# Mixer of a decoder trunk: the loads that bring queries and keys back are issued by SP instead of GpSimd

## The chip, the cores and the metric

The kernel runs on one core of one Trainium2 chip. The metric is the device time of one execution in microseconds (us). The core has a matrix engine (PE; its weight loads are listed apart as PEld), a vector engine (DVE), a scalar engine (ACT), a general engine (GpSimd, listed as POOL) and SP, which computes nothing and issues transfers. Each engine works through its own list of instructions in order, and an instruction that waits holds up everything behind it on that engine. A transfer is issued by SP, ACT or POOL and then carried out by the core's 16 DMA engines; the issuer goes on at once, and a semaphore tells when the data has landed. What SP issues stands in the profile as queue q1 (hardware descriptors), what POOL issues as queue q0 (software descriptors).

## The reference

Two layers (DEPTH = 2) over x of 512 tokens by 1024 channels. Each layer is a half-step SwiGLU, a token mixer, and a second half-step SwiGLU, each followed by a layer norm. The mixer projects x by w_in and has three head groups, all causal:

```
aq, ak, av, bq, bk, bv, cc = split(x @ w_in[l])
o_a = rms_norm(diff_attention(rope(aq), rope(ak), av, lam))      # 6 heads, two maps of 32 channels each
o_b = rms_norm(dilated_attention(rope(bq), rope(bk), bv))        # 6 heads of 64 channels
o_c, v_first = rwkv7_mixer(cc, ...)                              # 4 heads, a recurrence over the tokens
x = layer_norm(ALPHA * x + concat(o_a, o_b, o_c) @ w_out[l])
```

diff_attention takes the softmax of two score maps per head and subtracts lam times the second from the first. All is float32.

## The kernel before, in words

Products are kept near float32 precision by splitting every operand into a rounded part (hi) and a remainder (lo) and adding three matmuls (`mm3`). Weights are loaded by SP (tiles `wr`, two buffers, in the mixer), split by ACT (`wh`) and POOL (`wl`), eight buffers each.

The mixer is written as streams (`RANK` lists them), Python generators that emit instructions piece by piece. A planner, `Board.merge`, keeps an estimated clock for each engine and always continues the stream that can run first by that estimate; so the order on every engine is fixed when the program is built, and the estimated cost of a transfer's issue (1.04 us on POOL, 0.47 us on SP) shifts it. The streams near the change are these.

`columns` projects x. For queries and keys it goes by pairs of heads: three pairs of group A, three of group B. A pair is projected for four tiles of 128 tokens and rotated.

`turner` transposes each such tile on PE, splits it into hi and lo in a tile `z` (ACT writes one part, DVE the other; `z` has two buffers), and SP stores it to DRAM (`qkA` or `qkB`, one tensor per pair). Four stores make a pair complete.

`fetch` (lines 769 to 798) loads a pair back, head by head (e = 0, 1), rearranged so that one matmul reaches hi and lo products together. A head of group A takes four loads: 64 partitions of `q` and 64 of `k` (256 KB each), whose source is two blocks of 32 rows, hi and lo or one of them twice; and 32 partitions of `q` and of `k` (128 KB each) from one block. A head of group B takes two loads into the two halves of `q` (256 KB each, 128 partitions, source two blocks of 64 rows) and one of 64 partitions into `k` (128 KB). The tiles `q` and `k` share four buffers (tag `x`), so two heads can be held at a time. The first head of a group also loads the mask (`bias`).

`attend` computes the scores of 24 units per group (three pairs, two heads, four query tiles): PE makes `p<-k,q`, DVE adds the mask and takes the maximum, ACT the exponential, PE transposes and multiplies with the values. It frees a head's `q` and `k` after the head's fourth unit.

`inside`, `invert`, `scan` and `rwkv_out` do the recurrence. `inside` sends its small blocks through DRAM on SP's queue (`ub`, then `tt` to `td` and back); `scan` loads `kr` on SP.

Of the kernel before, what the change touches and what calls it, by code (L numbers as in the profile page):

```python
# [520 lines left out]
class Mix:  # L521
# [246 lines left out]

    def fetch(self):

        dma = self.gps.dma_start
        ap = lambda t, off, dims: bass.AP(tensor=t.tensor, offset=t.offset + off, ap=dims)
        for grp in "AB":
            for hp in range(3):
                for e in range(2):
                    yield f"qk{grp}{hp}", "x", "x"
                    if (hp, e) == (0, 0):
                        yield f"qk{grp}{hp}", "x", "x", "bias"
                        self.bias = self.get("bias", "bias")
                        dma(self.bias, self.tr.consts[:, 130:642] if grp == "A" else self.tr.consts[:, 642:1154])  # L780
                    a = self.get("x", "q", (128, 2, S))
                    d = self.qk[grp, hp]
                    hi, lo, k = e * 64 * S, (256 + e * 64) * S, 128 * S
                    if grp == "A":
                        b = self.get("x", "k", (128, 2, S))
                        dma(a[0:64], ap(d, hi, [[256 * S, 2], [2 * S, 32], [1, 2 * S]]))
                        dma(b[0:64], ap(d, hi + k, [[0, 2], [2 * S, 32], [1, 2 * S]]))
                        dma(a[64:96], ap(d, hi, [[2 * S, 32], [1, 2 * S]]))
                        dma(b[64:96], ap(d, lo + k, [[2 * S, 32], [1, 2 * S]]))
                    else:  # L790
                        b = self.get("x", "k2", (64, S))
                        dma(a[:, 0, :], ap(d, hi, [[256 * S, 2], [S, 64], [1, S]]))
                        dma(a[:, 1, :], ap(d, hi + k, [[0, 2], [S, 64], [1, S]]))
                        dma(b, ap(d, lo + k, [[S, 64], [1, S]]))
                    self.qkt[grp, hp, e] = a.bitcast(FR), b.bitcast(FR)
                    self.mark(f"q{grp}{hp}{e}")
# [753 lines left out]
```

## Time and profile before

| what | value |
|---|---|
| runs | 2336.46, 2327.51, 2321.31 us; median 2327.51 us |
| the profiled execution's own time | 2319.83 us |
| its span, first to last instruction | 2318.0 us |
| PE / DVE / ACT / POOL busy | 96% / 49% / 35% / 14% |
| mean granted TensorE clock | 0.975 |
| mixer of layer 0, attention in it | about 385 to 815 us, 490 to 720 us |
| mixer of layer 1, attention in it | about 1532 to 1970 us, 1642 to 1875 us |

Times in the trace count from the span's start. A wait of an engine costs time only where nothing else was ready behind it in that engine's order, and on PE nearly every wait does. The profile lists for each transfer when it was issued and when it landed.

### The profile page before, as it was taken

What the parts mean: (1) busy time and instruction counts of PE and PEld (TensorE: products, weight loads), DVE (VectorE), ACT (ScalarE), POOL (GpSimd) and SP (SyncE); (2) the same over time, 40 slices, a digit from 0 to 9 for tenths busy, and PEclk for the clock granted to TensorE, in tenths of its full rate; (3) what the DMA queues carried; (4) which work ended last, traced back from release to release, by engine and by line L of the source; (5) the groups of instructions that cost most, each with busy time, mean ns of one, the idle gap of its engine ahead of it and who ended that gap; (6) DMA issues with size and microseconds to landing.
All of it is one profiled execution on the core that took longest, in us unless ns stands there. A gap on an engine that the chain in (4) does not pass through costs nothing.

```text
span 2318.0 us, 31736 instructions
## 1 busy us (share of the span) xinstructions
PE 2215.6 (96%) x12384; PEld 1863.6 (80%) x12384; DVE 1146.8 (49%) x2483; ACT 803.4 (35%) x1559; POOL 317.5 (14%) x344
## 2 busy tenths in 40 slices
PE   9999999988899999999999999999878999999998
PEld 8888888787776788888888888887877867888886
DVE  3333346766566633333653332656765666333336
ACT  4322223435444323222433222343444443222222
POOL 1000002343232200000010000033432322000000
PEclk9999999999899999999999999999987999999999
DMA  5333344354433323332543333432553323233334
GB/s 171 101 102 98 113 137 146 102 136 98 104 106 101 118 74 94 98 99 91 173 120 108 101 96 109 155 128 85 136 108 94 107 95 119 84 98 91 100 109 154
DMA packets 253030, 258.34 MB, mean 111 GB/s; under 512 B 45562, under 2 KB 202304, under 8 KB 252880
## 3 DMA queue, kind: packets, MB, share of 16 engines
q1 hardware_dynamic: 221488, 228.20, 32.4%
q0 software_dynamic: 30816, 27.06, 4.8%
q8 instruction: 97, 1.59, 0.3%
q10 hardware_dynamic: 576, 1.05, 0.1%
q14 instruction: 53, 0.43, 0.1%
HBM read 233.85 MB, written 22.28 MB: 110 GB/s over the span
## 4 chain that ended last, share of the span: by engine, by line
PE 80%; DVE 8%; DMA 5%; issue 4%; POOL 1%; ACT 1%; SPq 0%; POOLq 0%; DVEq 0%; ACTq 0%
PE p L87 18%; PE p L86 18%; PE p L85 18%; PE p L511 13%; PE m L511 4%; PE r L511 3%; DMA k<-qkA 3%; PE r L86 2%; PE r L85 2%; PE r L87 2%; DMA k<-qkB 1%; DVE x L511 1%; POOL wl L511 1%; DMA q<-qkB 0%; DVE x L146 0%
## 5 line engine op out<-in xcount | busy, mean ns | idle before, releaser
L80 DVE TENSOR_TENSOR lo<-raw,hi 128x1024 fp32r<-128x1024 f32 x300 | 366.2, 1223 | 627.8 <-ACT hi L79 627.5
L87 PE MATMUL p<-xhi,lo 128*128 128x512 f32 (+1 forms) x1392 | 535.7, 385 | 0.0
L86 PE MATMUL p<-xlo,hi 128*128 128x512 f32 (+1 forms) x1392 | 533.7, 383 | 0.7 <-DVE xlo L126 0.7
L85 PE MATMUL p<-xhi,hi 128*128 128x512 f32 (+1 forms) x1392 | 533.6, 383 | 0.5 <-ACT xhi L125 0.5
L79 ACT CAST hi<-raw 128x1024 fp32r<-128x1024 f32 x300 | 315.6, 1053 | 583.5 <-PE p L86 258.1
L86 PEld LDWEIGHTS p<-xlo,hi 128*128 128x128 f32 x1392 | 261.7, 188 | 56.3 <-DVE xlo L126 1.1
L85 PEld LDWEIGHTS p<-xhi,hi 128*128 128x128 f32 x1392 | 261.8, 188 | 53.8 <-ACT xhi L125 1.0
L87 PEld LDWEIGHTS p<-xhi,lo 128*128 128x128 f32 x1392 | 261.9, 188 | 52.6
L511 POOL TENSOR_TENSOR wl<-wr,wh 128x512 fp32r<-128x512 f32 x152 | 203.8, 1360 | 670.1 <-ACT wh L511 629.3
L511 PE MATMUL p<-wh,xhi 128*128 128x256 f32 (+1 forms) x704 | 233.7, 332 | 1.4 <-DVE rb L511 1.1
L511 PE MATMUL p<-wh,xlo 128*128 128x256 f32 (+1 forms) x704 | 218.9, 311 | 0.5 <-DVE xlo L511 0.4
L511 PE MATMUL p<-wl,xhi 128*128 128x256 f32 (+1 forms) x704 | 218.5, 310 | 0.0
L87 PE MATMUL p<-hi,hl 128*128 128x512 f32 x528 | 205.8, 390 | 0.0
L86 PE MATMUL p<-lo,hh 128*128 128x512 f32 x528 | 205.8, 390 | 0.0
L85 PE MATMUL p<-hi,hh 128*128 128x512 f32 x528 | 205.7, 390 | 0.0
L511 PEld LDWEIGHTS p<-wh,xhi 128*128 128x128 f32 x704 | 138.9, 197 | 12.7 <-PE p L511 1.5
L511 PEld LDWEIGHTS p<-wh,xlo 128*128 128x128 f32 x704 | 138.7, 197 | 7.6 <-DVE xlo L511 2.2
L246 DVE TENSOR_TENSOR hr<-p,hr 128x512 f32<-128x512 f32 x88 | 60.8, 691 | 167.3 <-PE p L87 156.9
L511 PEld LDWEIGHTS p<-wl,xhi 128*128 128x128 f32 x704 | 139.2, 198 | 4.3
L247 ACT CAST hh<-hr 128x512 fp32r<-128x512 f32 x88 | 54.3, 617 | 205.9 <-DVE hr L246 195.8
L511 ACT ACTIVATE t<-t,nm 128x128 f32<-128x128 f32 (+3 forms) x144 | 80.2, 557 | 125.0 <-DVE nm L511 124.0
L85 PEld LDWEIGHTS p<-hi,hh 128*128 128x128 f32 x528 | 99.1, 188 | 20.6
(253 smaller groups left out, 3061.0 us busy)
## 6 DMA issues: line engine op xcount, KB each, us to landing
raw<-in_ffn_a_down SPq DMA_DIRECT2D x66, 512.0 KB, 3.3
raw<-in_ffn_b_down SPq DMA_DIRECT2D x66, 512.0 KB, 3.3
raw<-in_ffn_a_gate SPq DMA_DIRECT2D x44, 512.0 KB, 3.8
raw<-in_ffn_a_up SPq DMA_DIRECT2D x44, 512.0 KB, 3.9
raw<-in_ffn_b_gate SPq DMA_DIRECT2D x40, 512.0 KB, 3.9
raw<-in_ffn_b_up SPq DMA_DIRECT2D x40, 512.0 KB, 3.8
wr<-in_w_in SPq DMA_DIRECT2D x56, 256.0 KB, 3.1
wr<-in_w_in SPq DMA_DIRECT2D x24, 512.0 KB, 3.8
```

What stands on the lines that cost most here:

```text
L79: nc.scalar.copy(hi, raw)
L80: (vec or nc.vector).tensor_tensor(lo, raw, hi.bitcast(FT), op=OP.subtract)
L85: mm(out, lh, rh, start=first, stop=False)
L86: mm(out, lh, rl, start=False, stop=False)
L87: mm(out, ll, rh, start=False, stop=last)
L246: nc.vector.tensor_tensor(hr, acc[1, f], hr, op=OP.mult)
L247: nc.scalar.copy(hi, hr)
L511: return call(*args, **kw)
```

## The change

The loads of `fetch` are issued by SP on its hardware queue. The mask load stays on GpSimd. All addresses, sizes and buffers are the same.

```diff
     def fetch(self):
 
-        dma = self.gps.dma_start
+        dma = self.sp.dma_start
...
                         self.bias = self.get("bias", "bias")
-                        dma(self.bias, self.tr.consts[:, 130:642] if grp == "A" else self.tr.consts[:, 642:1154])
+                        self.gps.dma_start(self.bias, self.tr.consts[:, 130:642] if grp == "A" else self.tr.consts[:, 642:1154])
```

The 42 loads of a layer move from POOL's list to SP's, and since the planner counts less for them, the order of the other streams shifts around them. Three places follow; the number behind a name tells one use of a buffer from the next.

SP in layer 0, around the first pair of group A, before: stores of the second pair (`qkA0_1`), then the recurrence's trip through DRAM (`td0`, `td`).

```order
L511 DMA qkA0_1_2685<-z_3877 128x4x128
L511 DMA qkA0_1_2685<-z_3951 128x4x128
L511 DMA qkA0_1_2685<-z_4003 128x4x128
L511 DMA td0_4051<-tt_3586 128x16x16 x2
L511 DMA td_4050<-td0_4051 128x1x256 x2
```

The same place now:

```order
L511 DMA q_3939<-qkA0_0_2684 64x1x1024
L511 DMA k_3940<-qkA0_0_2684 64x1x1024
L511 DMA q_3939<-qkA0_0_2684 32x1024
L511 DMA k_3940<-qkA0_0_2684 32x1024
L511 DMA q_3945<-qkA0_0_2684 64x1x1024
L511 DMA k_3946<-qkA0_0_2684 64x1x1024
L511 DMA q_3945<-qkA0_0_2684 32x1024
L511 DMA k_3946<-qkA0_0_2684 32x1024
L511 DMA qkA0_1_2685<-z_3951 128x4x128
L511 DMA wr_4021<-in_w_in 128x4x128 x2
L511 DMA qkA0_1_2685<-z_4003 128x4x128
L511 DMA td0_4069<-tt_3586 128x16x16 x2
```

Both heads of the pair are issued in one go, ahead of the second and third store of the next pair, a weight load and the recurrence's trip.

ACT in layer 0, between the third and the fourth unit of that pair's first head (`t` are the units' exponentials, `aT` a transposed unit, `wh` weights), before:

```order
L511 COPY aT_4125<-m_4123 128x128
L511 CAST wh_4142<-wr_3904 128x512
L511 CAST wh_4146<-wr_3904 128x512
L511 ACTIVATE t_4159,l_4156<-t_4159,nm_4160 128x512
L511 ACTIVATE t_4165,l_4156<-t_4165,nm_4166 128x512
```

and now:

```order
L511 COPY aT_4131<-m_4129 128x128
L511 CAST z_4133<-m_4134 128x256
L511 COPY v_4044<-p0_4046 128x2x128
L511 ACTIVATE t_4162,l_4159<-t_4162,nm_4163 128x512
L511 ACTIVATE t_4168,l_4159<-t_4168,nm_4169 128x512
```

The fourth tile of the second pair, `z_4133`, is now written ahead of the fourth unit's exponentials; before it (as `z_4183`) came behind them. It takes the buffer of `z_3951`, whose store stands right behind the eight loads on SP.

SP in layer 0, from the second to the third pair of group B, now (before, SP had the stores and the weights alone, and POOL the loads):

```order
L511 DMA qkB0_2_2689<-z_6344 128x4x128
L511 DMA q_6382<-qkB0_1_2688 128x1x512 x2
L511 DMA k2_6383<-qkB0_1_2688 64x512
L511 DMA q_6387<-qkB0_1_2688 128x1x512 x2
L511 DMA k2_6388<-qkB0_1_2688 64x512
L511 DMA qkB0_2_2689<-z_6415 128x4x128
L511 DMA qkB0_2_2689<-z_6469 128x4x128
L511 DMA wr_6531<-in_w_out 128x2x512
L511 DMA qkB0_2_2689<-z_6541 128x4x128
L511 DMA wr_6607<-in_w_out 128x2x512
L511 DMA q_6633<-qkB0_2_2689 128x1x512 x2
L511 DMA k2_6634<-qkB0_2_2689 64x512
```

Here the second store of the third pair, `z_6415`, stands right behind two heads' loads; the fourth, `z_6541`, takes its buffer.

## Rows read from the trace of the kernel before

**Rows 1.** Page, section 1, PE: busy us (share of span), instructions.

```profile
PE 2215.6 (96%) x12384; PEld 1863.6 (80%) x12384; DVE 1146.8 (49%) x2483; ACT 803.4 (35%) x1559; POOL 317.5 (14%) x344
```

**Rows 2.** Waits of PE, 385 to 815 us: us in total, times, longest.

```profile
PE p L511 <- DMA k<-qkA: 18.1, 3, 8.6
PE p L511 <- DMA q<-qkB: 1.7, 2, 1.2
```

**Rows 3.** Waits of PE, 1532 to 1970 us.

```profile
PE p L511 <- DMA k<-qkA: 20.6, 3, 11.5
```

**Rows 4.** Windows: stretch, length, engines' busy us, granted clock, DMA share, GB/s.

```profile
490.00:720.00 230.00, 199.93 (x1761) 177.56 (x1761) 149.77 (x561) 111.89 (x378) 73.67 (x85) 0.91 0.43 112
506.00:509.00 3.00, 2.98 (x14) 3.00 (x15) 1.20 (x7) 1.10 (x5) 0.00 (x0) 0.50 0.45 92
```

**Rows 5.** Timeline of PE: start, duration, instruction, count [idle before <- releaser].

```profile
506.02 0.76 PE L511 MATMUL p<-k,q 96*128 96x256 f32 x2 [3.50 <-DMA k<-qkA]
...
515.90 0.40 PE L511 MATMUL p<-k,q 96*128 96x256 f32 x2
...
545.05 0.77 PE L511 MATMUL p<-k,q 96*128 96x256 f32 x2 [8.60 <-DMA k<-qkA]
...
703.25 0.35 PE L511 MATMUL p<-q 128*128 128x256 f32 x1
```

**Rows 6.** Chain that ended last: start, us, what (a transfer runs from issue to landing).

```profile
494.42 11.35 DMA k<-qkA
...
528.26 16.54 DMA k<-qkA
...
576.00 12.29 DMA k<-qkA
...
704.07 8.25 DMA k<-qkB
```

**Rows 7.** Timeline of POOL: its issues of the loads (start, us, count).

```profile
492.56 0.69 POOL L511 DMA_DIRECT2D q<-qkA  x1 [1.57 <-issue]
...
526.40 0.72 POOL L511 DMA_DIRECT2D q<-qkA  x1
...
670.64 1.62 POOL L511 DMA_DIRECT2D q<-qkB  x2 [3.70 <-DMA qkB<-z]
...
694.13 1.62 POOL L511 DMA_DIRECT2D q<-qkB  x2 [1.53 <-PE m L511]
...
702.47 1.62 POOL L511 DMA_DIRECT2D q<-qkB  x2 [6.16 <-PE m L511]
```

**Rows 8.** DMA issues, whole program: issuer, count, KB each, median us to landing.

```profile
q<-qkB POOLq DMA_DIRECT2D x24, 256.0 KB, 9.3
...
ub<-am SPq DMA_DIRECT2D x64, 4.0 KB, 1.5
```

**Rows 9.** Windows while a head of group B is loaded; columns as in rows 4.

```profile
700.00:701.00 1.00, 1.00 (x10) 0.90 (x8) 0.34 (x5) 0.98 (x5) 0.00 (x0) 1.00 0.26 102
701.00:702.00 1.00, 1.00 (x7) 0.61 (x5) 0.28 (x1) 0.59 (x2) 0.00 (x0) 1.00 0.26 102
```

**Rows 10.** DMA issues, 492 to 497 us; columns as in rows 8.

```profile
qkA<-z SPq DMA_DIRECT2D x2, 256.0 KB, 12.3
q<-qkA POOLq DMA_DIRECT2D x2, 256.0 KB, 11.1
```

**Rows 11.** Timeline of SP: start, us from the first issue to the last.

```profile
511.06 1.77 SPq L511 DMA_DIRECT2D td<-td  x2
...
518.16 0.37 SPq L511 DMA_DIRECT2D qkA<-z  x1
...
689.98 0.36 SPq L511 DMA_DIRECT2D qkB<-z  x1
```

**Rows 12.** Timeline of ACT around the first pair's units.

```profile
500.18 0.37 ACT L511 CAST z<-m 128x256 fp32r<-128x256 f32 x1 [3.64 <-DMA qkA<-z]
...
512.28 0.24 ACT L511 COPY aT<-m 128x128 f32<-128x128 f32 x1
```

## The prediction, made before the result was known

> **What bounds the kernel now.** I read the busy table first [rows 1]: PE is busy 96% of the span, so time can only come from, or go into, stretches where PE stands still or runs at half clock. Then PE's waits inside the two mixers [rows 2, 3]: of all that PE waits for there, the loads this change moves are the largest item, 18.1 + 1.7 us in layer 0 and 20.6 us in layer 1. The attention stretch [rows 4] shows the frame, in its first row: PE busy 199.93 of 230 us at a mean clock of 0.91. The timeline of PE [rows 5] shows where the waits stand: 3.50 us before the first head of group A, 8.60 us before the third; in layer 1 the longest is 11.5 us [rows 3]. After such a wait the granted clock stays at 0.50, the lower of its two levels (1.2 of 2.4 GHz), for about 3 us [rows 4], the second row, which costs some 1.5 us more. Last the chain of waits [rows 6]: every link that is a load of this kind runs 8 to 17 us from issue to landing. So the loads' latency matters, and whatever makes the first head of a pair land earlier or later moves the kernel almost one for one.
>
> **Price of one load.** While one head of group B is being loaded, two big pieces of 256 KB move, and the DMA share stands at 0.26 with 102 GB/s [rows 9]. 0.26 of 16 engines is 4.2 engines: two per big piece, each at 102/4.2 = 24.5 GB/s. So the pieces whose source is two blocks go through two engines only, and one takes 262 KB / (2 x 24.5 GB/s) = 5.35 us. On POOL's queue the two pieces use different engines and run side by side. A 128 KB piece, spread over 16 engines, takes 131 KB / (16 x 24.5) = 0.33 us. What remains of the 9.3 us landing [rows 8] is 3.95 us of start and landing on POOL's queue; SP's smallest transfers land in 1.5 us [rows 8], which I take as start and landing there.
>
> No row shows which engines SP's queue gives to a two-engine piece. The bounds: always the same pair, so that pieces run one after another, or a different pair each, as on POOL's queue. I take the same pair, since every other SP transfer of this kernel starts from a fixed split and nothing in the trace shows SP's queue rotating. The Trainium skill, DMA: Bandwidth & Descriptors, section Why a DMA increments its semaphore by 16 and not by 1, says that a hardware-queue transfer uses as many engines as divide the slowest dimension on both sides, and always the lowest-numbered ones, while the software queue moves a cursor on. By that rule two-block pieces all meet on two engines; no run here shows it yet.
>
> Head of group B on SP: 2 x 5.35 + 0.33 + 1.5 = **12.5 us**, against 702.47 to 712.32 = 9.85 us now [rows 6, 7]; spread it would be 7.2 us. Head of group A: one big piece takes between 5.35 us and 11.1 - 3.95 = 7.15 us [rows 8, 10], two small ones 0.66: 12.9 to 16.5 us, and I take **14 us**, nearer the lower end, since the upper was measured with eight pieces in flight. Now: 492.56 to 505.77 = 13.2 us for the first head and 526.40 to 544.80 = 18.4 us for the third [rows 6, 7]. A second head issued at once lands 11 (B) to 12.5 us (A) after the first. So the first head of a pair comes about as late as today; what changes is how long the two engines stay taken: 26 us for a pair. Every other SP transfer is spread over all the engines, those two included, and lands only when they are free. Today such a store already takes 12.3 us behind a pair [rows 10].
>
> **The sum, layer 0.**
> 1. First pair (A). First head +0.8 us. Second head lands at 492.6 + 26.5 = 519, needed at 515.90 [rows 5]: up to +3. The store of `z_3951` stands behind the pair and lands near 520; ACT's `z_4133` needs that buffer, and in the new order it comes right behind the copy that ends at 512.5 [rows 12]. ACT stands there until 520, where it now waits at most 3.64 us, with the fourth unit's exponentials behind it: **+6.6 us**, which covers the other two.
> 2. Second pair, first head. The recurrence's loads, now issued at 511.06, follow a store that lands near 520, so go out near 521; the fourth store, now at 518.16 [rows 11], at about 524, landed at 526. So the load is issued when it is today, 526, but lands at 540 instead of 544.80. PE, 6.6 us late, would arrive there at 543 and finds it: the 8.60 us wait goes. Shift so far 6.6 - 8.6 = -2; some wait is likely left, so **-1 us**. In layer 1, with 11.5 us to absorb, -4.
> 3. Third pair: 12.29 us plus 1.86 for the three issues ahead of it [rows 6, 7] is 14.1 now, 14 then: 0. A held store there: +1.
> 4. First pair of B: its first head comes up to 12.5 - 9.85 = 2.7 us later; today's PE waits for such loads are 1.7 us in all [rows 2], so most of it lies beside other work: +0.5.
> 5. Second and third pair of B. The third pair's fourth tile uses the buffer of a store that stands behind two B heads issued at 670.64; these hold the engines until 670.64 + 1 + 22 = 694, landing near 696 instead of today's store time of 689.98 [rows 7, 11]. The third pair is then complete near 699.5 rather than 694: its first head lands at 712 against 703.66, its second, behind it on the same two engines, at 722 against 712.3. PE needs the first at 703.25 [rows 5]: **+10 us**.
>
> Layer 0: -1 + 1 + 0.5 + 10 = +10.5; layer 1: +7.5. The profiled execution took 2319.83 us and would take 2338; it lies 7.7 us under the median of the runs, so the forecast is 2327.5 + 18 = **2346 us**. POOL's part: it loses 42 issues of 0.5 to 0.8 us a layer, beside idle time (14% busy), so 0. SP gains them at about 0.4 us; what stands behind is told above. The mask load stays on POOL and costs nothing new.
>
> **Rivals.**
> A, faster: SP's queue gives each piece its own engines. A head of A then lands in 5.35 to 7.15 + 0.66 + 1.5 = 7.5 to 9.3 us, of B in 7.2. That is 4 to 9 us under today, which takes nearly all of the 18.1 + 1.7 and 20.6 us and about 9 us of half-clock time: up to -49. With a third lost to the next wait (PE idles for a dozen other releasers too), -33: 2294 us. For it: those waits end last on PE. Against: nothing in the trace shows a rotation on SP's queue. Chance 0.17. The Trainium skill, same page, section Issuing engine by pattern, recommends SP for simple loads; by that advice this case would be the likely one, and nothing measured here supports it for two-block pieces.
>
> B, clearly slower: stores and weights held behind the pairs decide. A pair of A at the upper price takes 2 x (14.3 + 0.66) + 1.5 = 31 us, and four pairs a layer each hold the third or fourth next `z` (two buffers), `td`, `kr` and `wr` by 10 to 19 us more than the 12.3 of today. If one such hold of 8 us is waited for at each of the four pairs, it is 4 x 8 x 2 = +64: 2392 us. It decides when the tile two stores on is due within some 25 us of a pair's issue; today's stores come 5 to 20 us apart. Chance 0.33.
>
> C, nothing: the lost latency and the absorbed waits cancel: 2327. Chance 0.15. My forecast, mild loss: 0.35, own range 2330 to 2362.
>
> **Numbers.** About 1% (23 us) is what a measurement of this kernel tells from no change. Faster by more: nearly all of A, 0.15. Slower by more (over 2351): B and 0.4 of the forecast, 0.47. The same: 0.38. The range leaves out the better half of A and the upper end of B: 2298 to 2396.
>
> **What would show it.** After the change, in the windows while a head is loaded and nothing else moves, a DMA share near 0.13 (two engines) for twice as long proves the shared pair; 0.26 proves rival A. Landing times of q and k: 6 to 12 us staggered within a head (shared), or all near 8 (spread). The `z`, `wr` and `td` transfers behind a pair landing after 20 us or more. PE's wait before the third head of A gone or small, ACT's wait for `z` near 515 us, a later fetch and a PE wait in the third pair of B. If ACT and PE never wait for these stores, steps 1 and 5 are wrong and C or A remains; if PE's waits for `k<-qkA` grow, my 14 us is too low.

## The result, and the profile after

The changed kernel takes 2403.64 us (median; 2400.95 to 2408.03) beside 2326.45 us for the kernel before on the same chip: a ratio of 1.033, 95% interval [1.029, 1.037]. It is slower by 77 us where 18 were forecast, and lies above the range. The profiled execution took 2405.72 us, its span is 2403.9 us against 2318.0, and the mean granted clock 0.945 against 0.975. The busy row of the page, beside [rows 1]:

```profile
PE 2266.4 (94%) x12384; PEld 1905.5 (79%) x12384; DVE 1138.5 (47%) x2483; ACT 806.8 (34%) x1559; POOL 261.2 (11%) x260
```

The same 12384 multiplications keep PE busy 50.8 us longer, and the rest of the span, in which PE stands idle, grew from 102.4 to 137.5 us. So of the 85.9 us between the two spans (the medians differ by 77), **35 are waiting and 51 are slower work**. Added up over the clock's records, PE's clock was at the lower level for 109 us in 16 stretches before and for 259 us in 26 after. PE was busy in 88 us of the former and in 202 us of the latter; at 1.00 in place of 0.50 half of that time would do, so the difference is worth 57 us by this estimate, and the clock accounts for all of the slower work.

The waits of all engines in the mixer of layer 0 (385 to 860 us of the changed kernel), those that a DMA ends, beside [rows 2]; then PE's longest in layer 1 (1582 to 2056 us), beside [rows 3]:

```profile
PE p L511 <- DMA k<-qkA: 19.6, 3, 6.9
PE p L511 <- DMA q<-qkB: 15.7, 4, 5.6
ACT z L511 <- DMA qkB<-z: 7.4, 1, 7.4
...
ACT z L511 <- DMA qkA<-z: 4.7, 1, 4.7
```

```profile
PE p L511 <- DMA k<-qkA: 23.0, 3, 8.1
```

Group A's waits are about what they were; group B's went from 1.7 to 15.7 us in layer 0 and are 1.5 us in layer 1. The waits of ACT for a store (`qkA<-z`, `qkB<-z`) go on to PE, since the copy that PE needs stands behind `z` in ACT's list. Two waits of PE in layer 0 and one in layer 1 come from this; in the kernel before they are 0.7 us or nothing:

```profile
PE m L511 <- ACT aT L511: 5.7, 1, 5.7
PE p L511 <- ACT v L511: 3.1, 1, 3.1
...
PE m L511 <- DVE z L511: 6.8, 1, 6.8
```

So of the 35 us of waiting about 19 are loads (40.4 us for q and k in both mixers before, 59.8 after) and about 16 are held stores. The attention stretch of layer 0 in the windows, beside [rows 4], and the one of layer 1:

```profile
495.00:762.00 267.00, 218.78 (x1757) 195.08 (x1758) 144.54 (x560) 113.87 (x378) 44.95 (x43) 0.81 0.31 96
```

```profile
1692.00:1956.00 264.00, 220.22 (x1760) 194.15 (x1760) 148.94 (x565) 114.64 (x380) 47.84 (x44) 0.82 0.32 98
```

They take 267 us where it took 230 and 264 where it took 233, and PE's clock stands at 0.81 on average in layer 0 where it stood at 0.91. Two windows of 1 us in which nothing but heads moves (last two columns: DMA share, GB/s), beside the 0.26 and 102 GB/s of [rows 9]:

```profile
514.00:515.00 1.00, 1.00 (x7) 1.00 (x6) 0.04 (x1) 0.46 (x3) 0.00 (x0) 0.50 0.13 53
...
703.00:704.00 1.00, 0.00 (x0) 0.00 (x0) 0.98 (x2) 0.00 (x0) 0.13 (x1) 0.50 0.13 51
```

A share of 0.13 is two of 16 engines, at 53 and 51 GB/s: one piece at a time, 262 KB / 51 GB/s = 5.1 us each. The forecast of the shared pair holds, and so does its price. SP's own timeline (start, duration, instruction), first pair of group A from its fifth load on:

```profile
499.79 0.51 SPq L511 DMA_DIRECT2D q<-qkA  x1
500.40 3.06 SPq L511 DMA_DIRECT2D k<-qkA  x1
503.50 4.95 SPq L511 DMA_DIRECT2D q<-qkA  x1
508.50 0.88 SPq L511 DMA_DIRECT2D k<-qkA  x1
509.48 0.38 SPq L511 DMA_DIRECT2D qkA<-z  x1
512.03 7.83 SPq L511 DMA_DIRECT2D wr<-in_w_in  x2
519.95 0.46 SPq L511 DMA_DIRECT2D qkA<-z  x1
520.50 6.25 SPq L511 DMA_DIRECT2D td<-tt  x2
```

Here is something that the forecast did not have, and an issuer does not always go on at once: the sixth and the seventh load's issue take 3 and 5 us instead of 0.4 to 0.6. SP stands in its own issues while the two engines work off what is queued, and so does everything behind it in SP's list. By the semaphore events the pair issued from 497.57 us on landed at 512.59 (first head) and 523.98 (second), 15.0 and 26.4 us after its issue began, and the store of `z_3951`, issued at 509.48, at 524.69.

PE's timeline where it waits for a head in layer 0, beside [rows 5] (start, duration, instruction, idle time before it and what ended it):

```profile
512.63 0.80 PE L511 MATMUL p<-k,q 96*128 96x256 f32 x2 [6.74 <-DMA k<-qkA]
...
550.53 0.77 PE L511 MATMUL p<-k,q 96*128 96x256 f32 x2 [5.91 <-DMA k<-qkA]
...
608.36 0.55 PE L511 MATMUL p<-k,q 96*128 96x256 f32 x1 [6.94 <-DMA k<-qkA]
...
660.63 0.55 PE L511 MATMUL p<-q 128*128 128x256 f32 x1 [4.58 <-DMA q<-qkB]
...
706.79 0.55 PE L511 MATMUL p<-q 128*128 128x256 f32 x1 [4.97 <-DMA q<-qkB]
...
750.29 0.55 PE L511 MATMUL p<-q 128*128 128x256 f32 x1 [5.56 <-DMA q<-qkB]
```

Cut at the first scores of the same heads, and taken from the windows view of both kernels, layer 0 reads:

| stretch of layer 0 (us in it, PE busy) | before | after | more idle | more busy |
|---|---|---|---|---|
| mixer's start to first head of A | 121.0, 110.3 | 125.6, 112.2 | 2.7 | 1.9 |
| first to third head of A | 39.0, 28.8 | 37.9, 28.9 | -1.3 | 0.1 |
| third to fifth head of A | 43.5, 37.5 | 57.8, 50.2 | 1.6 | 12.7 |
| fifth of A to first of B | 42.2, 38.6 | 40.5, 39.5 | -2.5 | 0.8 |
| first to third head of B | 53.6, 50.9 | 57.9, 46.7 | 8.6 | -4.2 |
| third to sixth head of B | 27.5, 25.9 | 43.5, 32.3 | 9.6 | 6.4 |
| sixth head of B to the end | 103.2, 94.5 | 111.7, 102.3 | 0.7 | 7.8 |

The planner moved work between neighbouring stretches, so single rows mix both effects; the sums, 19.3 us more idle and 25.7 us more busy, don't. The last two stretches of the kernel before and then of the changed one (length; busy time of PE, PEld, DVE, ACT, POOL; granted clock):

```profile
684.34:711.81 27.47, 25.85 (x180) 19.75 (x178) 18.28 (x83) 20.48 (x70) 10.68 (x12) 1.00 0.37 109
711.81:815.00 103.19, 94.49 (x559) 77.31 (x560) 70.46 (x194) 35.02 (x81) 24.91 (x23) 0.98 0.34 110
```

```profile
706.79:750.29 43.50, 32.29 (x142) 24.91 (x143) 12.82 (x56) 19.14 (x65) 3.57 (x4) 0.70 0.34 110
750.29:862.00 111.71, 102.33 (x558) 84.34 (x559) 70.74 (x189) 35.22 (x79) 25.04 (x23) 0.88 0.29 93
```

In the first of them PE does fewer multiplications (142 against 180) in more busy time, at a clock of 0.70 instead of 1.00. In the last it does the same work, 558 against 559, and takes 7.8 us longer for it at 0.88 instead of 0.98.

### The profile page after: what moved, and what is told of

Read it like the earlier page. It is cut to its first block, busy times and chain, and to the rows that moved or that the text cites. A ratio compares the mean times of both kernels' runs of the same rounds, so it can differ in the third digit from the quotient of the medians.

```text
span 2403.9 us, 31738 instructions
## 1 busy us (share of the span) xinstructions
PE 2266.4 (94%) x12384; PEld 1905.5 (79%) x12384; DVE 1138.5 (47%) x2483; ACT 806.8 (34%) x1559; POOL 261.2 (11%) x260
## 4 chain that ended last, share of the span: by engine, by line
PE 80%; DVE 9%; DMA 6%; issue 2%; SPq 2%; ACT 1%; POOL 0%; DVEq 0%; ACTq 0%; POOLq 0%
PE p L87 17%; PE p L86 17%; PE p L85 17%; PE p L511 14%; PE r L511 5%; PE m L511 4%; DMA q<-qkB 2%; SPq L511 2%; PE r L86 2%; PE r L87 2%; PE r L85 2%; DMA qkA<-z 1%; DMA qkB<-z 1%; DVE x L511 1%; DMA k<-qkA 1%
## 5 line engine op out<-in xcount | busy, mean ns | idle before, releaser
L511 PE MATMUL p<-wh,xhi 128*128 128x256 f32 (+1 forms) x704 | 240.1, 341 | 6.6 <-ACT v L511 3.1
L511 PEld LDWEIGHTS p<-wh,xlo 128*128 128x128 f32 x704 | 142.7, 203 | 8.5 <-DVE xlo L511 2.9
L86 PEld LDWEIGHTS p<-lo,hh 128*128 128x128 f32 x528 | 99.1, 188 | 20.5
```

Of the source, the lines that this page charges most:

```text
L86: mm(out, lh, rl, start=False, stop=False)
L511: return call(*args, **kw)
```

## The experiments

The theories: **T1**, a piece whose source is two blocks moves through two engines, on SP's queue always the same two, and that makes the heads of a pair late and holds what is queued behind. **R1**, the loss is the planner's other order (it counts 0.47 us for an issue on SP, 1.04 on GpSimd). **R2**, SP's queue is slower for such loads whatever their source. **R3**, the number of loads or the order made of it decides. **T2**, the granted clock carries the larger part of the loss.

**The split on SP.** Each two-block load becomes two loads of one block, for group A (`b` and group B likewise):

```diff
-dma(a[0:64], ap(d, hi, [[256 * S, 2], [2 * S, 32], [1, 2 * S]]))
+dma(a[0:32], ap(d, hi, [[2 * S, 32], [1, 2 * S]]))
+dma(a[32:64], ap(d, lo, [[2 * S, 32], [1, 2 * S]]))
```

> The changed kernel, but each piece whose source is two blocks is written as two loads of one block each (six loads per head of group A, five per head of B, all on SP's queue). T1 (each two-block piece goes through two engines, all pieces through the same two, so that a pair of heads takes 26 us there, holds SP's other transfers and stops SP's issues): a head lands in 3 to 5 us, SP's stores are held no longer, PE's waits for q and k in layer 0 (35.3 us in the changed kernel) fall under 8, and the time falls below the kernel before: 2270 to 2310 us. R1 (the other order that the planner makes of it costs the time): the order is nearly as in the changed kernel, so it stays near 2400. R2 (SP's queue or its in-order waits are what is slow, whatever the source): near 2400, or more by the added issues.

Measured: 2271.81 us, ratio to before 0.976 [0.972, 0.979]: 5.5% under the changed kernel and faster than both. The transfers of 495 to 760 us (KB each, median us to landing):

```profile
q<-qkB SPq DMA_DIRECT2D x24, 128.0 KB, 2.7
qkA<-z SPq DMA_DIRECT2D x9, 256.0 KB, 3.7
q<-qkA SPq DMA_DIRECT2D x18, 128.0 KB, 4.9
k<-qkA SPq DMA_DIRECT2D x18, 128.0 KB, 4.8
```

PE waits for no load of q or k in either mixer. R2 is out, for more loads go through the same queue. R1 and R3 are not, as the order differs.

**One block, the same loads, on SP.** In the changed kernel only the source patterns are altered; the rows behind the first block are read in place of the second block:

```diff
-dma(a[0:64], ap(d, hi, [[256 * S, 2], [2 * S, 32], [1, 2 * S]]))
+dma(a[0:64], ap(d, hi, [[2 * S, 64], [1, 2 * S]]))
```

> The changed kernel with the same number, size and order of loads on SP, but the source of each two-block piece is one block of as many rows (it reads the rows behind the block in place of the second block, so what is computed of the scores is other data). T1 (two engines for a two-block source, all pieces on the same two): the pieces go to all the engines, a head lands in 3 to 5 us, the time is that of the split, 2265 to 2290. R3 (the split gained by its finer loads or by the order that the planner makes of more loads, not by the engines): above 2330.

Measured: 2266.98 us, ratio 0.973 [0.968, 0.978]. The lists of PE, DVE, ACT and POOL are the changed kernel's word for word; only the pattern of the source differs, and it is worth 137 us. R3 is out. Busy row and transfers, 495 to 760 us:

```profile
PE 2206.7 (97%) x12384; PEld 1856.2 (82%) x12384; DVE 1137.8 (50%) x2483; ACT 802.6 (35%) x1559; POOL 262.2 (12%) x260
```

```profile
q<-qkB SPq DMA_DIRECT2D x12, 256.0 KB, 3.3
...
q<-qkA SPq DMA_DIRECT2D x6, 256.0 KB, 5.0
k<-qkA SPq DMA_DIRECT2D x6, 256.0 KB, 5.5
```

Of the 132.6 us between the spans (2403.9 and 2271.3), 59.7 are busy time and 72.9 idle time.

**One block on GpSimd.** The same edit in the kernel before.

> The kernel before, loads on GpSimd's queue as they are in number, size and order, but the source of each two-block piece is one block of as many rows (other rows are read, so what is computed of the scores is other data). PE's waits for q and k should vanish as they did in the split on GpSimd's queue. T1 with idle time alone: the 29 us of PE's idle time that the split on that queue took away come off, without its added issues: 2285 to 2305. T2 (the granted clock takes back what the waits give, as in that split, where PE's busy time rose by 39 us): 2320 to 2350, with 170 us or more at the lower clock.

Measured: 2273.59 us, ratio 0.976 [0.971, 0.981], better than T1's own figure; T2's warning was wrong here, the time at the lower clock fell to 68 us. With sources of one block the two queues cannot be told apart (2267 and 2274). The orders differ between these two runs; in one and the same order, split loads take 2347 us on GpSimd's queue and 2348 on SP's (the split in the other orders, below). The two-block source costs 55 us on GpSimd's queue and 137 on SP's: **the change made an old flaw dearer**, it did not bring a new one.

**Order and queue apart.** The first keeps the changed order with GpSimd as issuer, the second the order of before with SP:

```diff
-dma = self.sp.dma_start
+dma = Watched(self.board, "sp", self.nc.gpsimd).dma_start
```

```diff
-dma = self.gps.dma_start
+dma = Watched(self.board, "pool", self.nc.sync).dma_start
```

> The changed kernel's order of the work (the planner counts the loads as SP's), but the loads are issued by GpSimd on its own queue, as before. T1: within 12 us of the kernel before, 2315 to 2340. R1 (the order costs it): most of the 77 us is here, 2380 to 2405. R2: as T1.

> The order of the kernel before (the planner counts the loads as GpSimd's), but SP issues them on its hardware queue. T1: the pair of engines decides, so most of the loss is here: 2380 to 2420. R1: near 2327. R2: 2380 to 2420 as T1; what tells R2 from T1 is the split of the sources, not this run.

Measured: 2345.27 us, ratio 1.007 [1.004, 1.011], for the order alone, and 2370.68 us, 1.016 [1.011, 1.020], for the queue alone, both just outside T1's figures. So the order costs 18 us with the loads on GpSimd and 33 with them on SP; the queue 43 in the old order and 58 in the new one. R1 holds some of the loss, though not as R1 has it: with one-block sources the new order is not slower (2267 against 2274). There is no one price for an order: below, split loads on SP take 2272 us in one order and 2348 in another, with no head late in either.

**Group A or group B alone split**, on SP (edits as in the split, in one branch):

> The changed kernel with the split (one block to a load) in group A alone; the heads of group B still go through two engines. By the split of both groups (2272) and none (2404) there are 132 us to share. T1, by where the shifts stand in the profile of the changed kernel (about half in group A's heads, half in group B's): 2325 to 2350. By the prediction's steps (group B's second and third pair carry the loss): 2360 to 2390, since the loss of B stays.

> The changed kernel with the split in group B alone; the heads of group A still go through two engines. T1: 2325 to 2350, the other half. By the prediction's steps (A costs 1 to 7 us, B 10 a layer): 2300 to 2320. If the two parts add up, this and the run with A alone split lie together 132 us under twice the changed kernel's time.

Measured: 2336.39 us, ratio 1.001 [0.998, 1.004], with A split; 2334.30 us, 1.004 [1.001, 1.008], with B split. Against the changed kernel they give back 67 and 69 us, some 137 together, where the full split gives 132. The halves are equal and add up. (The order moves a little with each split, in 487 and 75 of PE's 12384 places; the one-block run, in which it does not move, lies 5 us from the full split.) By the prediction's steps B should have carried nearly all; A's heads cost as much.

**Half the bytes**: the split for the pieces of k alone (`b` in group A, `a[:, 1]` in B).

> The changed kernel with the split for the keys' two-block pieces (group B: the second plane of q) alone, so half the bytes on the two engines: a head occupies them for 5 to 7 us, a pair for 11 to 14. In proportion to the bytes: 2338. T1 with a threshold (a pair that is done in 13 us comes sooner than the 15 us of a head now, and PE's waits for k go; the store behind it is due later): 2285 to 2315. If any sharing of the two engines costs the same: above 2360.

Measured: 2322.15 us, ratio 0.997 [0.994, 1.000]. None of the three: 62% of the 132 us came back for half the bytes, more than in proportion, less than with a threshold. PE still waits 6.8 us for k in layer 0.

**Held stores off SP.** First the z stores alone, then all of the mixer's transfers of data, then the weights too, are issued by GpSimd; PE, DVE and ACT keep the changed kernel's lists:

```diff
-sp.dma_start(self.qk[kind, i][:, :, :, t * 128:(t + 1) * 128].rearrange("a g p t -> p (a g) t"),
+Watched(self.board, "sp", self.nc.gpsimd).dma_start(self.qk[kind, i][:, :, :, t * 128:(t + 1) * 128].rearrange("a g p t -> p (a g) t"),
```

> The changed kernel with the stores of the transposed queries and keys (z) issued by GpSimd on its own queue, in the changed kernel's order; the loads stay as they are on SP. T1a (of the 77 us much is the z stores that stand behind a pair in SP's queue): ACT's and PE's waits for qkB<-z and qkA<-z go, a pair's heads still land 15 and 26 us after issue, the time falls by 20 to 40 us, to 2365 to 2385. T1b (the late heads decide, the stores only follow): within 12 us of the changed kernel, 2390 to 2415.

> The changed kernel with all of the mixer's transfers of data but the heads issued by GpSimd on its own queue (z, the decays' round trips td and ut, the kept kr, the values), weights still SP's; the order on TensorE, VectorE and ScalarE is the changed kernel's. What decides of the 77 us, transfers held behind the pairs or the heads' own late landing? Held transfers: with these free the kernel falls by 35 us or more, to 2340 to 2370. Late heads: as with z alone (2389), 2375 to 2400, with PE's waits for q and k still 20 us or more in layer 0.

> The same with the mixer's weights issued by GpSimd too, so that inside the mixer SP carries little but the heads and nothing of the layer's other work stands behind a pair. Held transfers: another 10 to 20 us below the run without the weights, 2325 to 2360. Late heads: within 10 us of that run, 2370 to 2400, and PE's waits for q and k stay.

Measured: 2389.19 us (ratio 1.025 [1.020, 1.031]), 2402.54 us (1.032 [1.026, 1.038]) and 2449.84 us (1.050 [1.047, 1.054]). The first is between its two figures; the second gives nothing back. PE's waits there, 385 to 880 us:

```profile
PE p L511 <- DMA k<-qkA: 20.0, 3, 10.6
PE p L511 <- DMA q<-qkB: 15.4, 5, 6.9
```

The three waits of PE behind held stores are gone in both runs (0.2 us is left for `aT` from ACT in layer 0, 1.2 in layer 1). Yet PE stands idle for 137.2 us of the span in the first and 142.7 in the second, where the changed kernel has 137.5: waiting for heads took their place (70.1 us for q and k in both mixers of the second run, 59.8 in the changed kernel). So the late heads suffice for the waiting, and freeing the stores in this way takes none of it away; the 14 us of the first run came out of PE's busy time (2254.4 us against 2266.4).

GpSimd's list is in order too, and as an issuer it has a price: the first pair of layer 0 is issued at 507.3 us in the second run and at 515.1 in the third, 497.6 in the changed kernel. The third run says nothing on the holds for this reason; PE's waits for q and k grew there to 50.5 us in layer 0. In the second this price may hide a gain, so what the held transfers would be worth with an issuer that is always free stays open.

**Filling the gaps.** Ahead of the first scores of each pair of heads in the changed kernel:

```diff
+if (e, qt, m) == (0, 0, 0):
+    for _ in range(16):
+        self.nc.tensor.matmul(sc[:, :128], tr.ident, tr.ident, start=True, stop=True)
```

> The changed kernel, order and loads untouched, but TensorE does 16 useless 128x128 multiplications of the identity (278 to 342 ns each in the profile of the changed kernel, so 3 to 5.5 us) ahead of the first scores of each pair of heads, where it waits 4.6 to 8.1 us for the loads in most pairs; their output is overwritten by the scores. The waits end when the loads land, so nothing gets shorter by this but the clock. T2 (of the 86 us between the two profiled executions, 51 us is PE at the lower clock, and the idle gaps ahead of the heads bring it on): the time at the lower clock falls from 259 us to 120 to 200, and the kernel, in spite of 36 to 66 us of added multiplications, is 10 to 40 us faster than the changed kernel: 2365 to 2393. Rival (these gaps do not bring it on): the time at the lower clock stays over 220 us and the kernel takes 2400 to 2430.

Measured: 2395.94 us, ratio 1.031 [1.026, 1.036], beside the changed kernel's 1.033 [1.029, 1.037]: no difference that these runs can tell, so the forecast of the time is missed. The busy row and the added multiplications:

```profile
PE 2288.4 (96%) x12768; PEld 1933.2 (81%) x12768; DVE 1136.0 (48%) x2483; ACT 806.0 (34%) x1559; POOL 261.2 (11%) x260
```

```profile
L1244 PE MATMUL p<-kept 128*128 128x128 f32 x384 | 46.1, 280 | 0.0
```

Without the 46.1 us added, PE is busy 2242.3 us, 24 less than in the changed kernel, with the same work; the time at the lower clock fell from 259 to 178 us, inside the forecast. So the gaps ahead of the heads do bring the lower clock on, for about half of the 51 us. PE's idle time fell from 137.5 to 98.5 us, so some 39 of the 46.1 us added stood where PE had waited and 7 came on top; the profiled execution is 17 us shorter than the changed kernel's, the median 8 us, which these runs can't tell from nothing.

**The split in the other orders.** The split on GpSimd (the kernel before with the split), and the split on SP in that order:

> The kernel before with the same split, loads still issued by GpSimd on its own queue. T1: the two-engine pieces are the price there too (5.35 of the 9.3 us that a head of B takes to land), so a head lands in 4 to 7 us, PE's waits for q and k (19.8 us in layer 0) fall by half, and the time falls by 15 to 40 us, to 2287 to 2312. R2 (GpSimd's queue, its start of about 4 us and its issues, is the larger part): no change within 10 us of 2327, since two more issues a head eat what the landing gains. R1 says nothing here: the order is about that of before.

> Split loads on SP's queue in the order of the kernel before (the planner counts them as GpSimd's). If the changed order is what helps once the pieces are spread: 2290 to 2320. If the order costs 10 to 17 us of its own, as it did with the loads on GpSimd: 2250 to 2262. If only the spread pieces on SP's queue matter: within 10 us of 2272.

Measured: 2346.54 us, ratio 1.007 [1.004, 1.010], and 2348.25 us, 1.008 [1.004, 1.011]. All figures were missed. Both have the same lists on PE, DVE and ACT, both wait for no load, and PE is idle only 73 and 72 us of the span; yet their medians are 75 and 76 us above the split on SP. Most of it is in the busy time: 2254.5 and 2269.8 us against 2205.9, which is 49 of 58 us and 64 of 72 between the profiled executions. Where the second lost it in layer 0 (PE busy second, granted clock third from the end):

```profile
684.00:688.00 4.00, 2.73 (x15) 1.68 (x15) 1.91 (x7) 1.66 (x6) 0.00 (x0) 1.00 0.23 70
688.00:700.00 12.00, 11.27 (x77) 8.60 (x76) 3.71 (x27) 3.05 (x12) 0.00 (x0) 0.53 0.38 110
700.00:712.00 12.00, 12.00 (x61) 9.32 (x61) 4.20 (x22) 5.43 (x18) 1.01 (x2) 0.50 0.00 1
712.00:724.00 12.00, 12.00 (x45) 9.47 (x44) 5.99 (x27) 6.09 (x24) 2.15 (x5) 0.50 0.33 116
```

What PE did before, from its timeline:

```profile
684.47 0.66 PE L511 MATMUL m<-kept,o 128*128 128x128 f32 x4 [0.75 <-ACT aT L511]
684.96 0.38 PE L511 MATMUL m<-kept,yc 128*128 128x128 f32 x2
686.09 0.50 PE L511 MATMUL p<-wh,xhi 128*128 128x512 f32 x1 [0.75 <-ACT xhi L511]
...
687.31 0.33 PE L511 MATMUL m<-uv,am 128*64 128x64 f32 x2
687.57 0.33 PE L511 MATMUL m<-st,kr 64*64 64x64 f32 x2
```

After two gaps of 0.75 us and in multiplications 64 wide the clock falls at 689 us and stays at 0.50 for 37 us, while PE is listed as busy nearly all of the time. Why it stays down so long in this order and comes back after 14 us or less everywhere in the split on SP is open. It belongs to the order that the planner makes when it counts these many loads as GpSimd's, not to a queue.

**The version to keep** is the split on SP, 2271.81 us, faster than the kernel before by 2.4% [2.1, 2.8].

## Why the prediction was wrong

**The mechanism held.** Pieces share two engines on SP's queue, at 5.1 us each where 5.35 was forecast. First heads of a pair landed 13.5 to 15.0 us after their issue (forecast 14 for A, 12.5 for B), and the second 11.2 to 13.0 after the first (forecast 11 to 12.5), 14.3 in the last pair, where it was issued 12 us behind. A pair's first piece landed 8 to 9 us after its issue, so start and landing took 3 to 4 us beside the 5.1; the 1.5 us of 4 KB transfers [rows 8] was too low for them, which is where group B's extra 1 to 2 us lie. The `z` stores landed late, 524.69 where 520 was said. The Trainium skill, DMA: Bandwidth & Descriptors, section Why a DMA increments its semaphore by 16 and not by 1, has the lowest-numbered engines for such a transfer on the hardware queue. The share of 0.13 agrees in that all pieces meet on the same two; which two they are no run here shows.

**Steps 2 to 4 failed: "The load is issued when it is today."** The sum set each landing against today's issue and let only the landing move. But a pair is issued when its last store is out and buffers are free, and both follow the pairs before. Issues of the six pairs of layer 0 came 5.0, 9.1, 19.7, 16.1, 22.6 and 29.4 us later than before (the first 5.0 are not the change's, see step 1). Step 2 forecast that the wait of 8.60 us before the third head goes: its load went out at 535.5 instead of 526, landed at 550.39, and PE waited 5.91 us. Step 3 forecast +1 and the fifth head came 19.8 us later than before, 14 more than the third. Step 4 took B's waits for small since they were 1.7 us; they became 15.7, and two of the four came before a second head (660.63, 750.29), which lands 25 to 28 us after the pair's issue and which these steps didn't cost.

**Step 1 named a hold that is there, and mis-sized it and what stands beside it.** The first head was 6.6 us late at PE and the second 12.3. 5.0 us of this lie ahead of the first moved load, where the change can't reach: PE's list is the same up to there, and the first pair is issued at 496.5 us in the one-block run on GpSimd too, which has the order of the kernel before, and at 492.6 in the profiled execution of the kernel before. The first head then landed 15.0 us after its issue instead of 13.2, where +0.8 was forecast. ACT stood at `z` for 4.7 us until 524.76, in place of at most 3.64 [rows 12], and PE waited 3.1 us for the copy behind it: that is the hold, with less than half of its +6.6.

**Step 5 named the right stretch and the right hold, and half the price.** Third to sixth head of B: 16.0 us longer, 9.6 of it idle, where +10 was forecast; the other 6.4 us are clock, with fewer multiplications in it. The idle time is not ahead of the fifth head, as forecast. It is 5.7 us behind ACT, which stood at `z` for a store behind two heads' loads, and 5.6 us ahead of the sixth head. In layer 1 the same hold cost PE 6.8 us.

**Rival B** rests on such holds. They reached PE at three of its eight pairs, with 15.6 us where it had 64. That its figure of 2392 was the nearest of all is luck in part: late heads and the clock made up the rest.

**The clock term was mis-sized most.** "About 3 us at 0.50, some 1.5 us more" was read from one wait [rows 4] and kept out of the sum of the steps; in the same trace the clock was at 0.50 for 10 to 14 us at a time around the later heads of group A. Stretches at the lower clock lasted up to 24 us in the changed kernel, 150 us more of them in all, and PE's busy time grew by 51 us, more than the 35 us of waiting. That the sum left this out, and that its waits were half of those measured, makes the 18 us forecast out of 77.

**Rival A** was refuted as to the queue. Its time, 2294, lies 22 us above what the same queue gives once the loads are split; that gain has another cause than A's, pieces that use all the engines.

## What to carry to other kernels

Before a transfer is moved to another queue, read how many engines it uses: the DMA share of a window in which it moves alone, times 16. Where the answer is two, make the source's outermost dimension long, here by splitting at the block, since with that done the queue made no difference (2347 and 2348 us in one order). Then time the whole kernel again, and not only the waits: the same split was 75 us slower in another order, with no load waited for. When waits on PE are priced, let the issue of the next load move with the lateness of the one before, and set PE's busy time at either level of the clock beside the idle time: here the slower work cost more than the waits.

## What the runs showed of the hardware

- Two 256 KB pieces of two blocks each ran side by side on GpSimd's queue (share 0.26) and one after the other on SP's (0.13). One-block pieces of the same size landed in 3.3 us (median, group B) and 5.0 to 5.5 us (group A) on SP's.
- SP's issue itself stood 3 to 5 us at the sixth and seventh load of a pair of group A, and 3.3 us at the third load of a head of group B (694.48 us), with two two-block loads ahead; SP's next transfers came later by it.
- The lower clock stayed for 37 us at 0.50 with PE listed as busy in 35.3 of the 36 us from 688 to 724, in a kernel that waits for no load. What kept it there is open.
- The Trainium skill, DMA: Bandwidth & Descriptors, section Rules for kernel authors, says that an outermost dimension of size c below 16 confines a transfer to at most c engines. The share of 0.13 for a source of two blocks agrees. The same section says that a transfer should not be split into halves by partition, as both halves use all 16 engines anyway. That reason does not hold where the whole uses two: here the halves took 132 us off the changed kernel.
